# Sixteen K tiles by Strassen in the head projections, weight sums of 1024 columns, and the decode step's dot products split between VectorE and ScalarE

## The chip, the cores and the metric

The kernel runs as one program on one core of a Trainium2 chip. The metric is device time in microseconds for one execution, inputs and outputs in HBM. Three timed executions of the kernel before gave 2168.1, 2169.01 and 2167.59 us; their median, 2168.1 us, is what a change is measured against. Engines are named as in the profile: PE (matmul), PEld (its weight load), DVE (VectorE), ACT (ScalarE), POOL (GpSimd, which here mostly issues transfers), SP (which issues the weight transfers).

## The reference, cut to what matters

One inference step of a two-layer trunk, for a prompt of 512 positions and 8 single decode positions that share all weights. All 520 positions go through the same projections; width is 2048, so K is 16 tiles of 128.

```
h = RMSNorm(x);  z = h @ W_in                     # 2048 x 8192, split into 8 parts of 1024
B, C, xc, g_conv | q, k, v, g_ret = split(z)
y_conv = B * conv3(C * xc) * silu(g_conv)
q, k = rope(q), rope(k) / 16                      # 4 heads of 256
o_n = sum_{m<=n} gamma^(n-m) (q_n . k_m) v_m      # prompt, in chunks
S = gamma * S + k^T v ;  o = q @ S                # each of 8 decode positions, its own state S (256 x 256 a head)
y_ret = GroupNorm(o) * silu(g_ret)
x = x + concat(y_conv, y_ret) @ W_out
x = x + sigmoid(x @ W_pg) * (p @ W_ple)           # then the next layer; a final RMSNorm at the end
```

The outputs are y for both groups and the new convolution and retention states. Everything is float32.

## The kernel before, in words

**Products.** float32 accuracy is had from three fp32r matmuls: an operand is split into a high part and a remainder, and `mm3` (L247 to L249) adds high x high, high x low and low x high in PSUM. Activations are kept transposed, 520 columns a tile, in two halves of 260; one such product is three matmuls of 128x128 weights and 260 columns. The high part of a weight is made by ACT (L229, a copy), the remainder by DVE (L230, a subtraction), both into a ring `split` of 60 column tiles of 128; the raw weights come by SP into a ring `raw` of 32 tiles.

**Pairs of output tiles.** Every projection is done two output tiles at a time. `plain` makes 16 K tiles x 2 output tiles x 2 halves x 3 = 192 matmuls. `strassen` treats s of the 16 K tiles (s even, q = s/2) as 2x2 blocks: two output tiles, two halves of K, two halves of the columns. It makes seven products of q tiles instead of eight, and does the other 16 - s tiles plainly at the end (the loop over `chunks(s, KT)`). Its seven products read weights directly or sums of weights; four sums a pair are made on DVE, in place in the raw ring (`add`, L319), in pieces of at most `CHA` = 4 tiles, so 512 columns. The parts of each product are split in pieces of at most 4 tiles. Where s is under 16 a fourth PSUM bank `c` is held for the plain tail and the second product is copied into it by ACT; with s = 16 that copy goes straight to the output slot, and there is one ACT copy fewer. The activation-side sums are made once per stage, four DVE operations of 260 columns for two K tiles (`operand_sums`), and split; they are built a few at a time between pairs.

**Stages.** In each of the two layers: 16 pairs for the four heads (q, k, v and gate of each), 16 for the convolution branch, 8 for W_out, 8 for W_pg (7 in the last layer, where the last two tiles are done in another form). The tables `HEADS`, `CONVS`, `OUT_ROWS` and `GATES` give s for each pair; the host packs the weights' K tiles in the order that s asks for. In the heads of layer 0 the first four pairs have s = 0, 0, 0 and 8, in layer 1 the first has 0; all other head pairs have 14, most convolution pairs 16.

**Beside the products.** In the heads, DVE does the rotation (L752 to L757), and pieces of the prompt's retention run through `later` and `middle`, small queues of closures that each pair empties at fixed points. The decode step is cut into 64 pieces, one for each layer, head and decode position: `sample_load` fetches the state (128 x 512) and the rows k and q spread over all partitions, `sample_step` scales the state by gamma on ACT (L776), adds k times v on DVE (L780, two halves of 256), writes the state out (L781), and takes the dot product of each half with q on DVE (L784: one multiply that also sums, and a read of the accumulator), into `osum`. `osum` is needed at the end of the convolution stage (`sample_norm`).

**Order.** The program is written in the order of its source; a scheduler then places the instructions of each engine by its own simulated times and by priorities (the splits and weight sums have a raised one). Each engine carries out its list in order. What an engine's list looks like is therefore read from the built program, and times from the trace.

Of the kernel before, what the change touches and what calls it, by code (L numbers as in the profile page):

```python
# [9 lines left out]
AF = mybir.ActivationFunctionType  # L10
ALU = mybir.AluOpType
MUL, ADD, SUB = ALU.mult, ALU.add, ALU.subtract

P = 128
# [3 lines left out]
SEQ = 512  # L18
NS = 8
T = SEQ + NS  # L20
# [9 lines left out]
NSLOT = 75  # L30
CH = 4
CHS = 4
CHA = 4
CHL = 4
CK = 256
BUSY = 10**9
# [13 lines left out]
EARLY = 6  # L50


HEADS = [[0, 0, 0, 8] + [14] * 12, [0] + [14] * 15]
CONVS = [[14] * 2 + [16] * 13 + [14]] * 2
OUT_ROWS = [[0, 8, 16, 16, 16, 16, 16, 0]] * 2

MIXED, MIX = 64, [*range(8, 14), *range(8), 14, 15]
# [22 lines left out]
class Slots:  # L80
# [18 lines left out]
    def put(self, *slots):  # L99
        for t in slots:  # L100
            self.free.append(self.used.pop(id(t))[1])
# [90 lines left out]
def trunk_kernel(  # L192
# [6 lines left out]
    V, S, G, PE, DMA = nc.vector, nc.scalar, nc.gpsimd, nc.tensor, nc.sync  # L199
# [33 lines left out]
    def chunks(a, b, most=CH):  # L233

        n = (b - a + most - 1) // most
        e = [a + (b - a) * i // n for i in range(n + 1)] if n else [a]
        return list(zip(e, e[1:]))
# [52 lines left out]
    def strassen(x, src0, src1, s, step=None):  # L290
# [24 lines left out]
        def add(out, x, y, op):  # L315
            for i, j in chunks(0, q, CHA):
                n = slice(P * i, P * j)
                with tc.high_priority(offset=WPRIO):
                    V.tensor_tensor(out[:, n], x[:, n], y[:, n], op)  # L319
# [243 lines left out]
    def norm_g(l, k):  # L563
        return vec[:, 16 * l + k : 16 * l + k + 1]
# [15 lines left out]
    def gam(h):  # L580
        return vec[:, 128 + h : 129 + h]
# [8 lines left out]
    osum = const.tile([P, 2, H, NS], F32, name="osum")  # L590
# [71 lines left out]
    def from_dram(src):  # L662
        def load(k):
            t = get()
            SIDE.dma_start(t, src[k])
            return t

        return load

    xs = []  # L670
    X = Operands(HEADS[0][2:] + CONVS[0], from_dram(xT), gain=lambda k: norm_g(0, k))
    X.todo = [t for t in ((i, False, True) for i in range(max(X.rows) // 2))]
# [43 lines left out]
    for l in range(DEPTH):  # L716
# [15 lines left out]
        def copied(ps):  # L732
            t = get()
            for n, v in zip((LEFT, RIGHT), ps):
                S.activation(t[:, n], v, AF.Copy)
            banks.put(*[v for v in ps if not any(v is o for o in over)])
            return Val(put, slot=t)
# [10 lines left out]
        def rope(z0, z1):  # L748

            a, b = ((z if z.ps is None else copied(z.ps)).slot for z in (z0, z1))  # L750
            t1, t2 = get(), get()
            V.tensor_tensor(t1, a, rc, MUL)  # L752
            V.tensor_tensor(t2, a, rs, MUL)
            V.tensor_tensor(a, b, rs, MUL)
            V.tensor_tensor(t1, t1, a, SUB)  # L755
            V.tensor_tensor(b, b, rc, MUL)
            V.tensor_tensor(b, b, t2, ADD)  # L757
            put(a, t2)
            return [t1, b]

        def silu(z):
            g = get()
            times(g, z, rb)
            z.done()
            S.activation(g, g, AF.Silu)
            return g
# [7 lines left out]
        def sample_step(h, b, st, kb):  # L774

            keep(S.activation(st[:, :512], st[:, :512], AF.Identity, scale=gam(h)))  # L776
            k = kb[:, 256:512]
            for e in range(2):
                c = slice(256 * e, 256 * e + 256)
                keep(V.scalar_tensor_tensor(st[:, c], k, vs[:, h, e, b : b + 1], st[:, c], MUL, ADD))  # L780
            SIDE.dma_start(o_rets[l, h, b], st[:, :512])  # L781
            for e in range(2):
                c = slice(256 * e, 256 * e + 256)
                V.tensor_tensor_reduce(k, st[:, c], kb[:, :256], 1.0, 0.0, MUL, ADD, osum[:, e, h, b : b + 1])  # L784
            put(st, kb)

        loaded = []
# [1 line left out]
        def sample():  # L789

            if loaded:
                sample_step(*loaded.pop(0))
            if todo:
                loaded.append(sample_load(*todo.pop(0)))
# [6 lines left out]
        def head(m):  # L801
            middle.append(lambda: X.fill(MORE_HEAD, 0))
            if m // 2 % 2:
                middle.append(sample)
            zs = pair(X, wi[l], m, m // 2 - skipped)
            X.fill(MORE_HEAD, 0)
            X.need(m // 2 - skipped + 1)
            sample()
            return zs

        def aside_copy(h, i, tiles):

            for d, t in enumerate(tiles):
                SIDE.dma_start(hs[l, h, i + d], t[:, :SEQ])  # L814
            put(*tiles)

        def retain(h):

            mt = 8 * h
            qks = small.tile([P, 4, 32], F32, tag="qks", name="qks")  # L820
            G.memset(qks, 0.0)


            if l == 0 and h == 0:
                q = rope(*first[:2])
            else:
                q = rope(*head(mt))
            for d in range(2):
                S.activation(qks[:, d, :NS], q[d][:, SEQ:T], AF.Copy)
            aside_copy(h, 0, q)  # L830


            if l == 0 and h == 0:
                kf = rope(*first[2:])
            else:
                kf = rope(*head(mt + 2))
            for d in range(2):
                S.activation(qks[:, 2 + d, :NS], kf[d][:, SEQ:T], AF.Copy)
            aside_copy(h, 2, kf)
            qkt = small.tile([P, 4, 32], F32, tag="qkt", name="qkt")  # L840
            V.transpose(qkt.rearrange("p a b -> p (a b)"), qks.rearrange("p a b -> p (a b)"))
            for g in range(4):
                SIDE.dma_start(kq[l, h, :, :, 32 * g : 32 * g + 32], qkt[32 * g : 32 * g + NS])


            vf = []
            for e, z in enumerate(head(mt + 4)):
                t = z.slot if z.ps is None else copied(z.ps).slot
                V.scalar_tensor_tensor(vs[:, h, e, :], t[:, SEQ:T], 1.0 / 16, rb[:, SEQ:T], MUL, MUL)
                vf.append(t)  # L850
            aside_copy(h, 4, vf)
            todo.extend((h, b) for b in range(NS))


            gts = [silu(z) for z in head(mt + 6)]
            for e, gt in enumerate(gts):
                S.activation(gs[:, 2 * h + e], gt[:, SEQ:T], AF.Copy)
            aside_copy(h, 6, gts)
            later.extend(steps(h))
# [190 lines left out]
        for h in range(H):  # L1050
            retain(h)
# [121 lines left out]
        if not tail:  # L1173
            X = Operands(HEADS[l + 1] + CONVS[l + 1], next_in, RESERVE_NEXT, gain=lambda k, l=l: norm_g(l + 1, k))
        for m in range(0, KT - tail, 2):
# [39 lines left out]
        if tail:  # L1215
# [30 lines left out]
            for j, n in enumerate(blocks):  # L1246
                c = slice(PC * j, PC * j + PC)
# [79 lines left out]
            for j, n in enumerate(blocks):  # L1327
# [18 lines left out]
                c, q = slice(PC * j, PC * j + PC), slice(j, j + 1)  # L1346
# [132 lines left out]
```

## Time and profile before

| | |
|---|---|
| timed runs | 2168.1, 2169.01, 2167.59 us; median 2168.1 us |
| the profiled execution, first to last instruction | 2167.3 us |
| PE busy | 2147.8 us (99%), 17861 matmuls |
| DVE busy | 1896.1 us (87%), 3849 instructions |
| ACT busy | 1264.5 us (58%), 2647 instructions |
| POOL busy | 430.6 us (20%) |
| transfers | 387.31 MB, mean 179 GB/s |

The span of the profiled execution is 0.8 us under the median of the timed runs. A row that groups instructions gives the line, the engine, the operation, out<-in, how many, then busy time and the mean duration of one, then how long the engine was idle before them and what released it. On DVE and ACT the durations of neighbours overlap, so that a stretch of work is shorter than their sum; the distance from one start to the next is what an instruction costs its engine.

### The profile page before, as it was taken

The numbers are of one execution on the slowest core, as the hardware profiler recorded it, in microseconds if no ns is written. First come the engines' busy times: TensorE is split into PE (matmuls) and PEld (weight loads), VectorE is DVE, ScalarE is ACT, GpSimd is POOL, SyncE is SP. The second block draws the span as 40 slices with busy tenths as digits, with TensorE's granted clock in tenths as the row PEclk, the third lists the DMA queues.
The fourth block names the chain that finished last, engine by engine and source line by source line (L and its number), as shares of the span: only waits on it lengthen the run. The fifth ranks groups of instructions, "written<-read, shape, count | busy, mean of one in ns | idle before, by whom it ended". The sixth has DMA issues, their size and how long they took to land. (4 is left out here: it accounts for less than half of the span.)

```text
span 2167.3 us, 48178 instructions
## 1 busy us (share of the span) xinstructions
PE 2147.8 (99%) x17861; PEld 2142.1 (99%) x17861; DVE 1896.1 (87%) x3849; ACT 1264.5 (58%) x2647; POOL 430.6 (20%) x746
## 2 busy tenths in 40 slices
PE   9999999999999999999999999999999999999998
PEld 9999999999999999999999999999999999999998
DVE  8889988998999987987997988989999998879884
ACT  8656655565555655655765655565645555456565
POOL 2313222211001211200212222231111022011011
PEclk9999999999999999999999999999999999999999
DMA  8555565545543745645645566664464355566455
GB/s 288 171 175 197 181 217 184 178 157 175 158 129 118 238 156 187 215 154 160 215 144 175 172 213 191 189 209 170 151 182 149 120 158 202 176 207 200 128 164 198
DMA packets 182861, 387.31 MB, mean 179 GB/s; under 512 B 25888, under 2 KB 56352, under 8 KB 182624
## 3 DMA queue, kind: packets, MB, share of 16 engines
q1 hardware_dynamic: 128704, 212.98, 31.6%
q0 software_dynamic: 53056, 169.84, 23.8%
q8 instruction: 140, 2.29, 0.4%
q10 hardware_dynamic: 864, 1.39, 0.2%
q14 instruction: 97, 0.79, 0.1%
HBM read 318.96 MB, written 65.15 MB: 177 GB/s over the span
## 5 line engine op out<-in xcount | busy, mean ns | idle before, releaser
L247 PE MATMUL ps_g<-slot,split 128*128 128x260 f32 x5465 | 1531.6, 284 | 7.2 <-ACT slot L307 2.9
L248 PE MATMUL ps_g<-slot,split 128*128 128x260 f32 x5465 | 1534.3, 282 | 0.3 <-DVE slot L555 0.3
L249 PE MATMUL ps_g<-slot,split 128*128 128x260 f32 x5461 | 1519.9, 283 | 0.5 <-DVE split L230 0.5
L229 ACT ACTIVATE split<-raw 128x512 fp32r<-128x512 f32 (+2 forms) x1347 | 777.3, 596 | 583.1 <-DVE raw L319 213.2
L247 PEld LDWEIGHTS ps_g<-slot,split 128*128 128x128 f32 x5465 | 1024.0, 188 | 10.1 <-ACT slot L307 3.7
L248 PEld LDWEIGHTS ps_g<-slot,split 128*128 128x128 f32 x5465 | 1028.5, 188 | 0.5 <-DVE slot L555 0.5
L249 PEld LDWEIGHTS ps_g<-slot,split 128*128 128x128 f32 x5461 | 1019.8, 188 | 1.0 <-DVE split L230 1.0
L230 DVE TENSOR_TENSOR split<-raw,split 128x512 fp32r<-128x512 f32 (+2 forms) x1346 | 849.2, 652 | 172.5 <-PE ps_g L248 85.4
L319 DVE TENSOR_TENSOR raw<-raw 128x512 f32<-128x512 f32 (+1 forms) x660 | 428.9, 660 | 32.5 <-DMA raw<-wi 23.7
L307 ACT ACTIVATE slot<-ps_g 128x260 f32<-128x260 f32 x336 | 127.4, 381 | 140.6 <-PE ps_g L249 122.7
L551 ACT ACTIVATE slot<-slot 128x520 fp32r<-128x520 f32 (+1 forms) x212 | 109.2, 562 | 46.6 <-DVE slot L414 11.1
L552 DVE TENSOR_TENSOR slot<-slot,slot 128x520 fp32r<-128x520 f32 (+1 forms) x212 | 124.4, 620 | 4.1 <-ACT slot L551 3.9
L781 POOL DMA_DIRECT2D o_rets<-slot x64 | 35.3, 552 | 351.6 <-DVE slot L780 131.7
L307 DVE TENSOR_TENSOR slot<-ps_g,slot 128x260 f32<-128x260 f32 x168 | 70.9, 424 | 6.0 <-PE ps_g L249 3.7
L869 POOL DMA_DIRECT2D slot<-hs x64 | 46.2, 724 | 118.7 <-DVE split L230 42.7
L814 POOL DMA_DIRECT2D hs<-slot x64 | 35.6, 556 | 139.3 <-DVE slot L755 61.3
L780 DVE SCALAR_TENSOR_TENSOR slot<-slot,vs,slot 128x256 f32<-128x256 f32 x128 | 56.1, 481 | 4.5 <-ACT slot L776 4.3
L746 DVE TENSOR_TENSOR slot<-slot,slot 128x520 f32<-128x520 f32 x80 | 55.8, 698 | 4.7 <-DMA o_rets<-slot 3.7
L770 POOL DMA_DIRECT2D slot<-sret x64 | 35.5, 554 | 114.6 <-ACT split L229 37.3
L1058 POOL DMA_DIRECT2D slot<-x1s x76 | 40.8, 538 | 87.6 <-PE ps_g L249 27.2
L1209 POOL DMA_DIRECT2D x2s<-slot x30 | 16.4, 545 | 201.6 <-DVE slot L1204 200.6
L771 POOL DMA_DIRECT2D slot<-kq x64 | 34.9, 547 | 106.0 <-DVE slot L876 22.2
(217 smaller groups left out, 1733.8 us busy)
## 6 DMA issues: line engine op xcount, KB each, us to landing
raw<-wi SPq DMA_DIRECT2D x377, 256.0 KB, 3.9
raw<-wo SPq DMA_DIRECT2D x128, 256.0 KB, 5.4
raw<-wg SPq DMA_DIRECT2D x122, 256.0 KB, 4.1
raw<-wi SPq DMA_DIRECT2D x136, 192.0 KB, 4.0
slot<-x1s POOLq DMA_DIRECT2D x76, 260.0 KB, 5.1
slot<-sret POOLq DMA_DIRECT2D x64, 256.0 KB, 4.0
hs<-slot POOLq DMA_DIRECT2D x64, 256.0 KB, 4.0
slot<-hs POOLq DMA_DIRECT2D x64, 256.0 KB, 5.2
```

What stands on the lines that cost most here:

```text
L229: S.activation(hi, raw, AF.Copy)
L230: V.tensor_tensor(lo, raw, F(hi), SUB)
L247: PE.matmul(out, wh, xh, start=start, stop=False, skip_group_check=more)
L248: PE.matmul(out, wh, xl, start=False, stop=False, skip_group_check=more)
L249: PE.matmul(out, wl, xh, start=False, stop=stop, skip_group_check=more)
L307: fn(*args)
L319: V.tensor_tensor(out[:, n], x[:, n], y[:, n], op)
L551: keep(S.activation(hi, src[:, n], AF.Copy))
L552: V.tensor_tensor(lo, src[:, n], F(hi), SUB)
L746: V.tensor_tensor(out[:, n], v, table[:, n], MUL)
L780: keep(V.scalar_tensor_tensor(st[:, c], k, vs[:, h, e, b : b + 1], st[:, c], MUL, ADD))
L869: SIDE.dma_start(t[:, :512].rearrange("p (m n) -> p m n", m=2), src)
```

## The change

Three tables and constants, and one function.

- `HEADS`: every 14 becomes 16 (12 pairs in layer 0, 15 in layer 1). `CONVS`: the first two pairs of each layer go from 14 to 16, the last stays at 14. That is 31 pairs.
- `CHA` = 8: a weight sum is one instruction of up to 8 tiles (1024 columns), in every pair with Strassen tiles.
- `sample_step`: the new state (512 columns) is multiplied by q in one DVE operation, with q read twice, and ACT adds up each half of 256 with a copy that accumulates. The rows k and q trade places in `kb`, so that the product can be written over both.

```diff
-CHA = 4
+CHA = 8
...
-HEADS = [[0, 0, 0, 8] + [14] * 12, [0] + [14] * 15]
-CONVS = [[14] * 2 + [16] * 13 + [14]] * 2
+HEADS = [[0, 0, 0, 8] + [16] * 12, [0] + [16] * 15]
+CONVS = [[16] * 15 + [14]] * 2
...
         def sample_step(h, b, st, kb):
 
             keep(S.activation(st[:, :512], st[:, :512], AF.Identity, scale=gam(h)))
-            k = kb[:, 256:512]
+            k, q = kb[:, :256], kb[:, 256:512]
             for e in range(2):
                 c = slice(256 * e, 256 * e + 256)
                 keep(V.scalar_tensor_tensor(st[:, c], k, vs[:, h, e, b : b + 1], st[:, c], MUL, ADD))
             SIDE.dma_start(o_rets[l, h, b], st[:, :512])
+            both = kb[:, :512].rearrange("p (e d) -> p e d", e=2)
+            V.tensor_tensor(both, st[:, :512].rearrange("p (e d) -> p e d", e=2), q.unsqueeze(1).broadcast_to([P, 2, 256]), MUL)
             for e in range(2):
-                c = slice(256 * e, 256 * e + 256)
-                V.tensor_tensor_reduce(k, st[:, c], kb[:, :256], 1.0, 0.0, MUL, ADD, osum[:, e, h, b : b + 1])
+                S.activation(both[:, e], both[:, e], AF.Copy, accum_out=osum[:, e, h, b : b + 1])
             put(st, kb)
...
             for d in range(2):
-                S.activation(qks[:, d, :NS], q[d][:, SEQ:T], AF.Copy)
+                S.activation(qks[:, 2 + d, :NS], q[d][:, SEQ:T], AF.Copy)
...
             for d in range(2):
-                S.activation(qks[:, 2 + d, :NS], kf[d][:, SEQ:T], AF.Copy)
+                S.activation(qks[:, d, :NS], kf[d][:, SEQ:T], AF.Copy)
```

In the changed kernel the lines from L783 on stand one lower.

Counted over the whole built program, the matmuls of 260 columns into `ps_g` go from 16311 to 16218. The weight sums (L319) go from 520 of 512 columns and 140 of 384 to 312 of 1024, 8 of 896, 4 of 768 and 12 of 512. The splits (L229 and L230, each) go from about 1031 of 512 columns, 249 of 384 and 66 of 256 to about 1248, 32 and 4. ACT has 31 copies of PSUM to PSUM fewer and 128 accumulating copies more.

On DVE, this is the middle of a head pair of layer 1 (the pair of v of the first head), before the change. `raw` holds weights and their sums, `split` the parts that PE reads.

```order
L319 TENSOR_TENSOR raw_72<-raw_72 128x384
L230 TENSOR_TENSOR split_73<-raw_72,split_73 128x384
L230 TENSOR_TENSOR split_73<-raw_72,split_73 128x512
L230 TENSOR_TENSOR split_73<-raw_72,split_73 128x384
L319 TENSOR_TENSOR raw_72<-raw_72 128x512
L230 TENSOR_TENSOR split_73<-raw_72,split_73 128x512 x3
L230 TENSOR_TENSOR split_73<-raw_72,split_73 128x384
L319 TENSOR_TENSOR raw_72<-raw_72 128x512
L230 TENSOR_TENSOR split_73<-raw_72,split_73 128x384
L230 TENSOR_TENSOR split_73<-raw_72,split_73 128x512 x2
L230 TENSOR_TENSOR split_73<-raw_72,split_73 128x256 x2
```

And this is the same place in the changed kernel.

```order
L230 TENSOR_TENSOR split_73<-raw_72,split_73 128x512 x2
L319 TENSOR_TENSOR raw_72<-raw_72 128x1024
L230 TENSOR_TENSOR split_73<-raw_72,split_73 128x512 x6
L319 TENSOR_TENSOR raw_72<-raw_72 128x1024
L230 TENSOR_TENSOR split_73<-raw_72,split_73 128x512 x6
L319 TENSOR_TENSOR raw_72<-raw_72 128x1024
L307 TENSOR_TENSOR slot47_858_14722<-ps_g_14718,slot47_858_14722 128x260
L319 TENSOR_TENSOR raw_72<-raw_72 128x1024
```

The sums are whole, the splits have one width, and the two splits of 256 that fed the plain tail of the pair are gone.

On ACT, this is a decode step of layer 1 (the state is in slot 897) before the change, from its scaling by gamma on; L307 empties PSUM banks.

```order
L776 ACTIVATE slot24_897_15905<-slot24_897_15905,vec_74 128x512
L307 ACTIVATE ps_g_16243<-ps_g_16241 128x260
L229 ACTIVATE split_73<-raw_72 128x384
L229 ACTIVATE split_73<-raw_72 128x512 x2
L229 ACTIVATE split_73<-raw_72 128x256
L307 ACTIVATE slot35_916_16244<-ps_g_16240 128x260
```

And this is the same step in the changed kernel, where L785 is the accumulating copy.

```order
L776 ACTIVATE slot33_897_15556<-slot33_897_15556,vec_74 128x512
L229 ACTIVATE split_73<-raw_72 128x512
L776 ACTIVATE slot42_914_15869<-slot42_914_15869,vec_74 128x512
L229 ACTIVATE split_73<-raw_72 128x512 x2
L307 ACTIVATE slot35_916_15880<-ps_g_15877 128x260
L229 ACTIVATE split_73<-raw_72 128x512
L785 ACTIVATE slot45_898_15557,osum_82<-slot45_898_15557 128x256 x2
L229 ACTIVATE split_73<-raw_72 128x512
L307 ACTIVATE slot35_916_15880<-ps_g_15879 128x260
```

The two sums come six instructions behind the scaling here; over the 64 steps it is between 3 and 22. Splits and PSUM copies stand behind them.

## The prediction, made before the change was run

> **What bounds the kernel now.** I read the engines' shares first, then PE's own waits, then windows over the stages that the change touches, and last what DVE and ACT wait for there. The page's first part:
>
> ```profile
> span 2167.3 us, 48178 instructions
> PE 2147.8 (99%) x17861; PEld 2142.1 (99%) x17861; DVE 1896.1 (87%) x3849; ACT 1264.5 (58%) x2647; POOL 430.6 (20%) x746
> ```
>
> PE is busy but for 19.5 us. A busy PE may still be a slow one, so the second view is the windows (length; then busy time and instructions of PE, PEld, DVE, ACT, POOL; granted clock; DMA share). The first is the W_out and W_pg stages of layer 0, with 16 Strassen tiles; then the heads of layers 0 and 1 and the late convolution pairs of layer 0:
>
> ```profile
> 760.00:1040.00 280.00, 280.00 (x2340) 280.00 (x2338) 236.02 (x432) 154.99 (x298) 38.75 (x73) 1.00 0.53 170
> 120.00:500.00 380.00, 379.06 (x3170) 378.81 (x3169) 346.09 (x757) 225.89 (x492) 96.64 (x164) 1.00 0.58 184
> 1130.00:1530.00 400.00, 399.33 (x3339) 398.83 (x3338) 355.57 (x777) 234.37 (x518) 98.68 (x170) 1.00 0.59 185
> 520.00:680.00 160.00, 160.00 (x1338) 160.00 (x1337) 146.82 (x283) 87.41 (x175) 17.42 (x22) 1.00 0.47 143
> ```
>
> In the first window 280 us hold 2340 matmuls of 260 columns: **119.7 ns** each, at a full clock. The convolution window gives 119.6 ns, with DVE at 92%. So PE runs at its own pace in every stage, and the number of matmuls sets the time. The heads lose 0.94 us (layer 0) and 0.67 us (layer 1) of PE time in all, with DVE at 91% and 89%.
>
> How much room DVE and ACT have there is told by what they wait for. These rows are the waits of layer 1's heads, 1130 to 1530 us (total, times, longest):
>
> ```profile
> ACT split L229 <- PE ps_g L248: 30.5, 38, 2.5
> ACT split L229 <- PE ps_g L249: 14.0, 13, 2.5
> DVE split L230 <- ACT split L229: 17.4, 23, 2.9
> DVE raw L319 <- DMA raw<-wi: 16.3, 13, 3.0
> DVE slot L307 <- PE ps_g L249: 1.8, 2, 1.5
> ```
>
> ACT stands 44.5 us because PE has not yet freed a place in the split ring: the weights are ready too early, not too late. DVE's waits for ACT are partly that same wait, passed on. A ring of 60 tiles holds seven chunks of four K tiles (high and low part each), and a chunk feeds 12 matmuls, so PE has 7 x 12 x 0.1197 = 10 us of work in store when the ring is full.
>
> **The change, part by part.** *Matmuls.* A pair with 14 Strassen tiles needs 7 x 7 x 3 = 147 and a plain tail of 2 x 4 x 3 = 24, so 171; with 16 it needs 7 x 8 x 3 = 168. 31 pairs change (12 + 15 head pairs, 2 x 2 convolution pairs): 93 fewer, which is also the difference in the built program (16311 to 16218). 93 x 119.7 ns = **11.1 us off PE**. Nothing hides it: PE is what ends last, and its weight loads go along one for one.
>
> [...]
>
> *Splits and weight sums on DVE.* What one costs is the distance between starts, since durations overlap. This is DVE's timeline in a stretch without idle time:
>
> ```profile
> 399.86 0.41 DVE L784 CUSTOM_DVE_ANT_0 slot<-slot,slot 128x256 f32<-128x256 f32 x1
> 400.20 0.08 DVE L784 DVE_READ_ACCUMULATOR2_ANT osum<- 128x1 f32 x1
> 400.20 0.55 DVE L230 TENSOR_TENSOR split<-raw,split 128x384 fp32r<-128x384 f32 x1
> 400.67 0.68 DVE L319 TENSOR_TENSOR raw<-raw 128x512 f32<-128x512 f32 x1
> 401.27 0.42 DVE L784 CUSTOM_DVE_ANT_0 slot<-slot,slot 128x256 f32<-128x256 f32 x1
> ```
>
> 256 columns cost 0.34 us, 384 cost 0.47, 512 cost 0.60: 0.13 us per 128 columns and 0.08 fixed. The trace has no sum of 1024 columns; on that line it costs 0.60 + 4 x 0.13 = 1.12 us. It can hardly be under 1.04 (the columns alone) or over 1.20 (two of 512); I take 1.12.
>
> A pair that goes from 14 to 16 had splits 7 x (0.47 + 0.60) + 2 x 0.34 = 8.17 us and has 14 x 0.60 = 8.40; sums 4 x (0.47 + 0.60) = 4.28 and now 4 x 1.12 = 4.48. That is **+0.43 us of DVE a pair**, 13.3 us for 31. The 47 pairs that had 16 already save 4 x (1.20 - 1.12) = 0.32 us each, 15.0 us, and three others 1.0 us together. In the heads alone it is 27 x 0.43 = +11.6 us, over windows in which DVE was idle for 78 us of 780. PE's store of 10 us covers it; bare, it would be those 11.6 us, less what the next part gives back.
>
> *Decode steps.* By durations the part looks large:
>
> ```profile
> L784 DVE CUSTOM_DVE_ANT_0 slot<-slot,slot 128x256 f32<-128x256 f32 x128 | 53.9, 421 | 0.0
> L784 DVE DVE_READ_ACCUMULATOR2_ANT osum<- 128x1 f32 x128 | 11.1, 87 | 0.0
> L230 DVE TENSOR_TENSOR split<-raw,split 128x512 fp32r<-128x512 f32 x1031 | 695.0, 690 | 147.8 <-PE ps_g L248 81.2 <-ACT split L229 51.8 <-issue 6.1
> ```
>
> 65.0 us go and 64 x 0.69 = 44.2 come. But the timeline shows that the accumulator reads cost no distance and the products 0.34 us, so a step saves 2 x 0.34 - 0.60 = 0.08 us of DVE, 5.1 us over 64. **DVE's sum** is 13.3 - 16.0 - 5.1 = about -8 us, off the path that sets the end. The product costs like the 512-column row as both read two SBUF operands; a repeated q might be slower, at most as much as today's two halves.
>
> ACT gets 128 accumulating copies of 256 columns, which the trace does not have. The nearest rows:
>
> ```profile
> L229 ACT ACTIVATE split<-raw 128x256 fp32r<-128x256 f32 x66 | 27.3, 415 | 36.7 <-DMA raw<-wi 29.0 <-PE ps_g L248 5.2 <-PE ps_g L249 1.9
> L988 ACT ACTIVATE slot<-slot,shift,rstp 128x256 f32<-128x256 f32 x6 | 3.2, 587 | 0.0
> L307 ACT ACTIVATE ps_g<-ps_g 128x260 f32<-128x260 f32 x121 | 45.1, 373 | 16.4 <-PE ps_g L249 16.1
> ```
>
> Below, 0.415 us (a plain copy); above, 0.587 + 0.087 us (two operands of a column each, and a read as long as DVE's). I take 0.50, nearer the copy that it is: +64 us (53 to 86), less 31 PSUM copies at 0.373 = 11.6 us. ACT goes from 1264 to about 1316 us, 61% of the span. That hides behind PE as long as ACT idles 44.5 us on a full ring in one stage.
>
> *The new wait.* L785 waits on ACT for DVE's product. Queued behind it are the high parts of the splits, for which DVE's remainder and then PE wait, and the copies out of PSUM. The tightest is the copy of bank `a` behind a pair's first product: the third product writes `a` again, so it may be late by the second product, 24 x 0.1197 = 2.9 us. DVE's own chain from the last L780 (0.34 us) to the product is 3 to 8 instructions, 1.5 to 4 us, and in most steps a dozen ACT instructions of about half a microsecond lie between. A handful of the 64 will make ACT stand 1 or 2 us, under the 2.9. I take nothing for it.
>
> *A sum that starts later.* One 1024-column sum needs both halves of its weights in, and its first split comes 1.12 - 0.60 = 0.52 us later. 10 us in store cover that too, except where PE has emptied the ring. PE's waits over the whole execution show how seldom that is:
>
> ```profile
> PE ps_g L247 <- ACT slot L307: 2.9, 4, 1.3
> PE ps_g L247 <- ACT ps_g L307: 1.6, 2, 1.2
> PE ps_g L247 <- ACT split L229: 1.5, 2, 1.3
> PE ps_g L249 <- DVE split L230: 0.5, 1, 0.5
> ```
>
> Three waits for splits in 2167 us, 2.0 us. [...]
>
> *Sum:* 2167.3 - 11.1 = 2156.2 us for the profiled execution; with the 0.8 us by which the median of the runs lies over it, **2157.0 us**. The decode step's transfers stay as they are; 62 weight transfers of 128 KB for the tails go into larger ones, and the bytes stay.
>
> **The rivals.**
>
> 1. *Fewer stalls as well* (2153.7 us). DVE gets lighter outside the heads, and the waits above (6.5 us for copies and splits) could shrink. For it: the convolution stages lose 0.32 us a pair. Against it: most of these waits stand at changes of stage, where the chain goes through ACT and transfers. Half of the 6.5 us gone is 3.3 us more.
>
> 2. *The heads empty the ring now and then* (2161 us). DVE's work per head pair rises by 0.43 us while PE's falls by 0.36. In bursts, such as a rotation (six operations of 520 columns, 0.61 us each on the line above) beside a wide sum that starts late, the 10 us run out. If a third of DVE's 11.6 us more in the heads gets through to PE, 3.9 us of the gain go back. For it: layer 1 already waits 16.3 us for weights. Against it: 44.5 us of ACT waiting on PE.
>
> 3. *ACT's queue blocks* (2167 us, no change). If the accumulating copies stop ACT long enough that PE loses 0.17 us a step, 64 x 0.17 = 11 us, the gain is gone. For it: 64 new waits in an in-order queue. Against it: L307's waits on PE's side come to 4.5 us today, though L776 and others wait in the same queue.
>
> 4. *DVE becomes the pace of all changed pairs* (2176 us, slower). Then the 93 matmuls buy nothing, and a changed pair costs DVE's 0.43 us: 13.3 - 5.1 = +8.2 us. It decides from the point where DVE has no idle time left in the heads: 44.4 of 400 us in layer 1 would have to be bound elsewhere. For it: of DVE's own waits there only the 1.8 us of L307 are on PE. Against it: the 92% window of the convolution, where pairs of 16 run at 119.6 ns.
>
> 5. *The change doesn't do what it says*: excluded for the matmuls, which are counted in the built program.
>
> **How the numbers follow.** The forecast (2156 to 2158.5) has 0.65, rival 1 has 0.10, rival 2 0.14, rival 3 0.07, rival 4 0.04. A measurement of this kernel tells about 0.2%, 4.3 us, from no change: faster is under 2163.8 us, slower over 2172.4. Faster is the forecast, rival 1 and nearly all of rival 2: 0.88. Same is rival 3 and the rest of rival 2: 0.08. Slower is 0.04. The range reaches from half of rival 1 (2154.5) to the bulk of rival 2 (2161.5); some 2 in 10 lie outside.
>
> **What would show it.** Right: PE busy near 2137 us and its idle time still near 19 us; windows in the heads with 119.7 ns a matmul; sums of 1024 columns with starts 1.12 us apart; DVE's busy time lower by about 8 us; ACT about 50 us busier. Wrong: PE waits on L229, L230 or L307 in the heads that total over 5 us (rival 2 or 3, by the line named), ACT idle before L785 for over 2.9 us at a time, or ACT's waits on PE in the heads gone (rival 4).

## The result and the profile after

The changed kernel took 2201.47 us (median of four runs, 2194.72 to 2206.27) against 2168.56 us before: a ratio of **1.0153**, 95% interval 1.0133 to 1.0173. Forecast was 2157.0 us. The change is slower by 33 us where it was to be faster by 11. Two single executions in the experiments below, one of e3 (4245 us) and one of d3 (2304 us), were in a slow state, and the medians given here are of the others.

The first lines of the page of the kernel after:

```profile
span 2200.2 us, 46804 instructions
PE 2156.1 (98%) x17768; PEld 2141.9 (97%) x17768; DVE 1898.6 (86%) x3271; ACT 1280.9 (58%) x2810; POOL 433.0 (20%) x746
```

The 93 matmuls are gone (17861 to 17768), and yet PE is busy 8.3 us longer and idle 44.1 us in place of 19.5. The three longest of PE's waits in the kernel after, whole execution (total, times, longest), name the engines:

```profile
PE ps_g L247 <- ACT slot L307: 13.6, 15, 3.0
PE ps_g L247 <- ACT split L229: 10.9, 13, 1.6
PE ps_g L249 <- DVE split L230: 4.7, 10, 0.6
```

Before, these were 2.9, 1.5 and 0.5 us. The windows that were shown of before, in the kernel after (length; busy time and instructions of PE, PEld, DVE, ACT, POOL; clock; DMA share):

```profile
120.00:500.00 380.00, 372.68 (x3072) 369.40 (x3071) 343.15 (x587) 229.97 (x530) 97.33 (x163) 1.00 0.55 182
1130.00:1530.00 400.00, 388.83 (x3193) 384.40 (x3193) 352.66 (x592) 236.65 (x540) 100.13 (x170) 0.99 0.56 183
520.00:680.00 160.00, 159.50 (x1328) 159.05 (x1328) 146.43 (x237) 90.66 (x208) 13.96 (x25) 1.00 0.46 146
```

The first two are the heads: 380 us of layer 0 now hold 3072 PE instructions where they held 3170, and 400 us of layer 1 hold 3193 in place of 3339. At 119.7 ns each that is 12.3 and 17.8 us lost, where it was 0.6 and 0.3. The convolution window loses 10 instructions, some 1 us. A second place lies behind the stages that the prediction looked at: the windows from the W_out stage of layer 1 to the end, of the kernel before and then of the one after, whose last 33 us are its longer time.

```profile
1760.00:2167.00 407.00, 396.32 (x3294) 394.93 (x3292) 327.57 (x622) 229.38 (x478) 68.30 (x126) 1.00 0.56 184
```

```profile
1760.00:2200.00 440.00, 424.25 (x3468) 421.70 (x3466) 344.10 (x611) 237.07 (x501) 74.73 (x128) 0.98 0.53 175
```

By the same price 12.7 us were lost there before and 24.9 after. So of the 44 us to be found (32.9 us between the profiled executions, and the 11.1 us of matmuls that were saved) the heads took 29.2 and this stretch 12.2. A single stall shows how, in lines of the timeline of the kernel after around 1240 us (lines between them are left out):

```profile
1239.76 1.67 ACT L229 ACTIVATE split<-raw 128x512 fp32r<-128x512 f32 x3 [2.07 <-DMA raw<-wi]
1240.44 0.39 PE L247 MATMUL ps_g<-slot,split 128*128 128x260 f32 x1 [1.57 <-ACT split L229]
1241.34 0.40 ACT L785 ACTIVATE slot<-slot 128x256 f32<-128x256 f32 x1
1241.74 0.40 ACT L785 ACTIVATE slot<-slot 128x256 f32<-128x256 f32 x1
1242.26 0.67 ACT L307 ACTIVATE slot<-ps_g 128x260 f32<-128x260 f32 x2
1242.98 0.58 PE L247 MATMUL ps_g<-slot,split 128*128 128x260 f32 x1 [2.03 <-ACT slot L307]
1243.36 0.42 PE L248 MATMUL ps_g<-slot,split 128*128 128x260 f32 x1
1243.58 0.42 PE L249 MATMUL ps_g<-slot,split 128*128 128x260 f32 x1
```

PE finds no split weights and waits 1.57 us. The first line's bracket says where this began: ACT itself had stood idle for 2.07 us until a transfer of raw weights landed. ACT then has three splits, two accumulating copies and only behind them the copy that frees PE's next PSUM bank, and PE waits another 2.03 us. From there the matmuls start 0.22 us apart instead of 0.12. Windows around that place show the granted clock with it (the third number from the right):

```profile
1232.00:1239.00 7.00, 6.88 (x58) 6.64 (x57) 6.43 (x12) 4.89 (x9) 1.33 (x2) 1.00 0.78 244
1239.00:1243.00 4.00, 0.53 (x3) 0.32 (x3) 3.65 (x7) 3.13 (x9) 0.73 (x1) 0.77 0.87 298
1243.00:1250.00 7.00, 7.00 (x40) 7.00 (x40) 5.56 (x10) 1.38 (x5) 1.71 (x4) 0.64 0.36 133
```

Behind the two waits, 3.6 us together, the granted clock is 0.64 in the mean of 7 us, which hold 40 matmuls where the 7 us ahead of the waits held 58. Other stalls begin at a transfer too. If each of PE's waits is followed back for 8 us through the waits of the engines in front of it, 9.9 of 35.8 us in the kernel after begin at late weights and 10.2 at other transfers; in the kernel before it is 2.0 and 3.3 of 11.2. These are estimates.

By kind, the 32.9 us are made up like this. Matmuls: -11.1. Idle time of PE: 44.1 - 19.5 = +24.6. Clock: its mean is 0.994 after and 0.999 before, so (1 - 0.994) x 2200 - (1 - 0.999) x 2167 = 13.2 - 2.2 = +11.0, an estimate. The clock's own records in the traces bear it out: half the clock was granted in the kernel after for 3.4 us from 162.5, 1804.4 and 1831.7 us on, for 6.8 us from 1241.2 and 2145.7 us on, and at the very end; in the kernel before at the very end alone. That is 13.6 us lost (1.4 of them while PE was idle anyway) against 1.6. The rest, 8.4, lies in PE's busy time, and the waits give it a size: the first matmul behind the wait above takes 0.39 us where the pace is 0.12, 0.27 more, and the times in PE's whole list of waits add up to 51 where they were 18; 33 x 0.27 = 8.9. That one matmul is typical: over the 34 waits that lie clear of each other and of the half clock, PE's busy time grows by 0.27 us a wait (median).

### The profile page after: what moved, and what is told of

It is laid out like the page before. It is cut to its first block, busy times and chain, and to the rows that moved or that the text cites. A ratio compares the mean times of both kernels' runs of the same rounds, so it can differ in the third digit from the quotient of the medians.

```text
span 2200.2 us, 46804 instructions
## 1 busy us (share of the span) xinstructions
PE 2156.1 (98%) x17768; PEld 2141.9 (97%) x17768; DVE 1898.6 (86%) x3271; ACT 1280.9 (58%) x2810; POOL 433.0 (20%) x746
## 5 line engine op out<-in xcount | busy, mean ns | idle before, releaser
L247 PE MATMUL ps_g<-slot,split 128*128 128x260 f32 x5434 | 1531.3, 285 | 29.2 <-ACT slot L307 13.6
L229 ACT ACTIVATE split<-raw 128x512 fp32r<-128x512 f32 (+1 forms) x1285 | 751.5, 620 | 489.4 <-PE ps_g L249 181.1
L230 DVE TENSOR_TENSOR split<-raw,split 128x512 fp32r<-128x512 f32 (+1 forms) x1284 | 837.5, 681 | 216.1 <-ACT split L229 119.6
L319 DVE TENSOR_TENSOR raw<-raw 128x1024 f32<-128x1024 f32 (+2 forms) x336 | 400.9, 1193 | 7.4 <-DMA raw<-wi 3.5
L307 ACT ACTIVATE slot<-ps_g 128x260 f32<-128x260 f32 x336 | 127.5, 381 | 202.7 <-PE ps_g L249 173.6
L307 DVE TENSOR_TENSOR slot<-ps_g,slot 128x260 f32<-128x260 f32 x168 | 70.6, 421 | 11.3 <-PE ps_g L249 11.3
L785 ACT ACTIVATE slot<-slot 128x256 f32<-128x256 f32 x128 | 51.6, 405 | 10.8 <-DVE slot L783 8.1
```

The lines of the kernel that those rows point to most:

```text
L229: S.activation(hi, raw, AF.Copy)
L230: V.tensor_tensor(lo, raw, F(hi), SUB)
L247: PE.matmul(out, wh, xh, start=start, stop=False, skip_group_check=more)
L307: fn(*args)
L785: S.activation(both[:, e], both[:, e], AF.Copy, accum_out=osum[:, e, h, b : b + 1])
```

## The experiments

Medians are given against the runs of the kernel before on the same chip, 2168 to 2169 us; a difference is to that.

**The three parts, each alone, and the change without its wide sums.** Three theories stood: the wide sums (W), 16 tiles in the heads (R), ACT's queue (S).

```diff
e1  HEADS, CONVS as in the change; CHA = 4, sample_step as before
e2  CHA = 8; the rest as before
e3  sample_step and qks as in the change; the rest as before
e4  the change with CHA = 4
```

> The tables of rows alone (31 pairs from 14 to 16 tiles), sums in pieces of 512 and the decode step as before. 93 matmuls fewer are worth 11.1 us. Theory W (the wide sums empty the split ring: a sum of 1024 columns, then ACT's high part, then DVE's remainder stand in a row before PE has work): no stall from this part, 2157 us, PE gaps as before. Theory R (16 tiles in the heads are too much for DVE beside the rotation and the retention): 2185 us or more, with gaps in 80 to 420 and 1120 to 1500 us and the half clock behind them. Theory S (the accumulating copies block ACT's queue): 2157 us.

> The weight sums of 1024 columns alone. No matmul goes. Theory W: 2185 us or more, since all 47 pairs of 16 tiles and the 384+512 pairs of the heads get the long chain. Theory R: 2168 us (no change), as DVE's work falls by some 15 us. Theory S: 2168 us.

> The decode step alone: one product on DVE, two accumulating copies on ACT. No matmul goes. Theory W and theory R: 2168 us, no change. Theory S: 2185 us or more, with PE waiting for L307 and L229 on ACT behind the accumulating copies.

> The change without its wide sums: tables and decode step, sums in pieces of 512 columns. Theory W: the whole gain stands, 2157 us. Theory R: 2185 us or more, as DVE's work in the heads is no less than with rows alone but for 5 us. Theory S: 2185 us or more.

| run | median us | ratio, 95% interval |
|---|---|---|
| e1, rows alone | 2187.83 | 1.0089, 1.0071 to 1.0107 |
| e2, wide sums alone | 2189.85 | 1.0102, 1.0087 to 1.0118 |
| e3, decode step alone | 2175.09 | 1.0031, 1.0017 to 1.0045 |
| e4, rows and decode step | 2182.75 | 1.0069, 1.0052 to 1.0086 |

Each part is slower alone: +19.6, +21.6 and +6.8 us. No theory stands as a single cause: W falls with e1 and e4, R with e2, S covers 7 us. PE's waits also differ in kind. For splits (L229 and L230) PE waits 2.5 us in the kernel before, 9.1 with rows alone and 15.6 in the change, but only 3.5 with wide sums alone. There the copies out of PSUM (L307) grew, from 4.7 to 9.9 us, and waits of other kinds from 4.1 to 10.1. Two rows of e2:

```profile
PE ps_g L247 <- ACT slot L307: 7.3, 10, 2.4
PE ps_g L247 <- ACT split L229: 1.4, 2, 0.8
```

The profile of e1 also upsets a reading. This is a row of ACT's waits in the heads of layer 1 (1130 to 1530 us), with rows alone:

```profile
ACT split L229 <- PE ps_g L249: 50.9, 45, 6.3
```

And this is the window over the same stretch:

```profile
1130.00:1530.00 400.00, 391.87 (x3256) 389.27 (x3255) 363.21 (x732) 224.45 (x460) 99.42 (x170) 1.00 0.57 185
```

ACT waits on a full ring for 50.9 us, more than the 44.5 of before, and in the same 400 us PE is idle for 8.1 us. A ring that is often full is no proof that it is never empty.

**Is it the order?** The scheduler places every instruction anew for each edit. Two edits that change no work (null edits) were made on both kernels.

```diff
n1, n3 (strassen)
-        z0, z1 = get(), get()
+        z1, z0 = get(), get()
n2, n4 (sample_step)
-            put(st, kb)
+            put(kb, st)
```

> The kernel before, with nothing of the change: the two output slots of a Strassen pair are taken in the other order (z1 before z0), so they swap places in memory. Same instructions, same sizes, same counts; in the built program 898 of 3851 DVE instructions and 717 of 2655 ACT instructions stand elsewhere. Theory O (the order on the engines: the order of before is a lucky one, and whatever moves it brings stalls of PE): 2175 to 2190 us, with PE gaps in the heads. Theory P (each part of the change has a price of its own in work or waits): 2168 us, within 4 us.

> The kernel before, with the two slots of a decode step given back in the other order (kb before st). Same work; 312 of 3851 DVE and 141 of 2655 ACT instructions stand elsewhere. Theory O: 2172 to 2185 us, less than the run above as less moves. Theory P: 2168 us, within 4 us.

> The changed kernel, with z1 taken before z0. Same work as the changed kernel; 845 of 3273 DVE instructions stand elsewhere. Theory O: another time than 2201 us, off by more than 5 us either way. Theory P: 2201 us, within 5.

> The changed kernel, with kb given back before st. Same work; 302 of 3273 DVE instructions stand elsewhere. Theory O: off 2201 us by more than 5 us, or not, but the four null edits together spread over 10 us or more. Theory P: 2201 us, within 5.

| | as it is | z1 before z0 | kb back first |
|---|---|---|---|
| kernel before | 2168.56 | 2187.04 (1.0091, 1.0067 to 1.0114) | 2167.80 (0.9999, 0.9990 to 1.0009) |
| kernel after | 2201.47 | 2226.11 (1.0272, 1.0256 to 1.0287) | 2210.34 (1.0192, 1.0175 to 1.0210) |
| difference | +33 | +39 | +43 |

Two slots that trade places cost 19 us on the kernel before and 25 on the one after, with not one instruction more; the other null edit costs nothing on the one and 9 us on the other. So a single comparison on this kernel carries some 20 us of order. And yet the change costs 33 to 43 us in all three columns, and the slowest of the three kernels before (2187 us) is 14 us faster than the fastest of the three after: in these orders it has a price of its own besides. In n3, PE's waits tell where the order hurts:

```profile
PE ps_g L247 <- ACT slot L307: 18.3, 15, 4.1
PE ps_g L249 <- DVE split L230: 14.0, 21, 1.9
```

The change with the slots exchanged waits longer for the same copies (13.6 us in the change as it is) and three times as long for low parts (4.7 us there).

**How much does DVE's work in the heads matter?** Four of the six operations of each rotation were left out, so that q and k are not rotated.

```diff
-            t1, t2 = get(), get()
+            t1 = get()
             V.tensor_tensor(t1, a, rc, MUL)
-            V.tensor_tensor(t2, a, rs, MUL)
-            V.tensor_tensor(a, b, rs, MUL)
-            V.tensor_tensor(t1, t1, a, SUB)
-            V.tensor_tensor(b, b, rc, MUL)
-            V.tensor_tensor(b, b, t2, ADD)
-            put(a, t2)
+            V.tensor_tensor(b, b, rs, MUL)
+            put(a)
```

> The kernel before with four of the six DVE operations of each rotation of q and k left out (two of 520 columns stay, so q and k are not rotated): 64 operations of 0.61 us, 39 us of DVE in the heads, 4.9 us a head. PE's work is the same. It is the control for the next three: 2166 to 2170 us by every theory but the order (up to 2187 by that alone).

> The tables of rows alone, with the same four operations of each rotation left out. Theory D (DVE has too little spare time in the heads: with 16 tiles its work for one matmul rises by 4 to 5%, and the store of split weights runs dry): the gain comes, 11 us under the control, about 2157 us, and the stalls of the heads (22 us with the full rotation) go. Theory L (it is the chain of sum, high part, remainder and PSUM copy through two in-order engines, not DVE's work): still 2180 us or more.

> The sums of 1024 columns alone, with the same four operations left out. Theory D: near the control, within 5 us. Theory L: 15 to 20 us over the control, with stalls outside the heads too (690 to 780 and 1760 to 1850 us).

> The whole change, with the same four operations left out. Theory D: about 2157 us, 11 us under the control. Theory L: 2190 us or more. Both in part: rows give their 11 us, wide sums take 15 to 20, so 2172 to 2180 us.

| with the light rotation | median us | against the light kernel before |
|---|---|---|
| kernel before (d1) | 2173.26 | |
| rows alone (d2) | 2174.21 | +1.0 (with the full rotation +19.6) |
| wide sums alone (d3) | 2192.41 | +19.2 (+21.6) |
| the change (d4) | 2193.22 | +20.0 (+33) |

The two parts behave differently. Counted with the 11.1 us of matmuls that they save, the rows cost 30.7 us with the full rotation and 12.1 when DVE has 4.9 us less to do in each head. That is what theory D says in part: their 11 us still do not come. PE idles 29.0 us in d2 and 26.1 in d1 (span less busy time of one execution each; that of d1 took 6 us over its median). The price of the wide sums does not care (theory L). But leaving out work moves instructions too: d1 has less to do and is 5 us over the kernel before, so order may have a part in these differences.

**Where the wide sums cost, and how deep the store is.** For this the lead was worked out: for each low part, the time from the end of its subtraction (L230) in the trace to the start of the first matmul that reads that place of the ring, which the built program gives. In us, the median and, behind the stroke, the value that a tenth of the parts fall short of:

| kernel | heads, layer 0 (80 to 500) | convolution (520 to 690) | W_out, W_pg (780 to 1050) | heads, layer 1 (1150 to 1500) |
|---|---|---|---|---|
| before | 7.8 / 4.7 | 3.4 / 2.0 | 7.6 / 5.0 | 6.1 / 2.7 |
| after | 5.7 / 2.0 | 3.3 / 1.1 | 7.2 / 3.6 | 6.0 / 1.8 |
| rows alone | 6.8 / 2.7 | 3.2 / 1.4 | 7.7 / 5.1 | 6.0 / 2.2 |
| wide sums alone | 6.9 / 2.9 | 3.0 / 1.0 | 7.3 / 3.5 | 6.1 / 2.2 |
| before, z1 before z0 (n1) | 6.3 / 2.2 | 3.2 / 1.8 | 7.1 / 4.6 | 5.4 / 2.0 |
| after, z1 before z0 (n3) | 4.0 / 0.9 | 3.2 / 1.3 | 7.4 / 3.6 | 3.7 / 0.9 |

PE's store is nowhere 10 us: 3 to 8 us, with dips to half of that and less. The wide sums take 1.0 to 1.8 us off its dips in three of the four stages and 0.5 in the last, and the rows 2.0 in the heads of layer 0. The dips do not say by themselves where time is lost, though. They are deepest in the convolutions, where the kernel after loses 1 us. With wide sums alone the heads of layer 0 lose 0.7 us (3169 matmuls in 380 us) at dips of 2.9, and those of layer 1 lose 10.4 us (3255 in 400) at dips of 2.2. Four runs tested whether the depth decides (theory T).

```diff
f1, f2 (strassen, L294 and L316)
-        q = s // 2
+        q, cha = s // 2, (CHA if x.gain else 8)     # f1: wide in W_out and W_pg only
+        q, cha = s // 2, (8 if x.gain else CHA)     # f2: wide in heads and convolutions only
-            for i, j in chunks(0, q, CHA):
+            for i, j in chunks(0, q, cha):
f3 (before)
-SPLIT = 60
+SPLIT = 52
f4 (e4: rows and decode step)
-SPLIT = 60
+SPLIT = 64
```

> The kernel before with sums of 1024 columns only in the W_out and W_pg stages (22 pairs), where the splits lie some 7 to 8 us ahead of PE. Theory T (a wide sum delays the next split by some 1.5 us, and that costs only where the store is thin): no change, 2168 us within 5. Theory O (order): up to 20 us either way, with stalls in the heads, which the edit does not touch.

> The kernel before with sums of 1024 columns (896 where s is 14) only in the heads and the convolution pairs, where the splits lie 3 to 8 us ahead with dips under 3. Theory T: all of the 20 us that the wide sums cost alone, 2183 to 2192 us, with the stalls in the heads of layer 1 and at the ends of the convolution stages. Theory O: anything from 2168 to 2190 us.

> The kernel before with a ring of 52 split tiles in place of 60: the same work, a store that is one chunk (1.4 us) shallower. Theory T (depth decides): 2180 us or more, the stalls in the heads. If depth does not matter but order does: anything, with no tie to the stages where the store is thin.

> Rows and decode step without wide sums (2182.8 us with a ring of 60), with a ring of 64: half a chunk, 0.7 us, deeper. Theory T: fewer stalls in the heads, 2165 to 2177 us. Theory O: between 2165 and 2200 us, with no direction.

| run | median us | ratio, 95% interval |
|---|---|---|
| f1, wide in W_out and W_pg | 2170.69 | 1.0008, 0.9998 to 1.0018 |
| f2, wide in heads and convolutions | 2188.84 | 1.0088, 1.0067 to 1.0109 |
| f3, before with 52 tiles | 2197.19 | 1.0131, 1.0116 to 1.0146 |
| f4, rows and step with 64 tiles | 2192.27 | 1.0100, 1.0083 to 1.0117 |

The first three went as T says. In f1 the dips of the lead fall from 5.0 to 3.1 us in the stages that were edited, and no time is lost: the same sums are free there. Nearly all of the price is in f2. And one chunk off the ring, with the same instructions, costs 28 us; PE's waits in f3:

```profile
PE ps_g L247 <- ACT slot L307: 10.3, 10, 2.4
PE ps_g L247 <- ACT split L229: 8.2, 10, 1.4
```

Both are the waits that the change made longer too (13.6 and 10.9 us there). None of the three excludes the order (theory O), since each edit also moved instructions. ACT's list has 2647 entries in all of these kernels; compared place by place in the traces (line, operation, names and shape), it differs from that of the kernel before in 265 places in f1 and 320 in the null edit n2, which are both free, in 566 in n1 (+19 us), and in 1017 in f2 and 1603 in f3. The two edits that cost 20 and 28 us are also those that moved most. (d1 moved 983 places and costs 5 us, with less to do.)

f4 went against T: it is 9.5 us slower than e4. The ring of 64 made the dips of the lead shallower in the convolutions (1.2 us in e4, 3.2 in f4) and in the heads (2.2 and 1.5 us in e4, 2.8 and 2.7 in f4; 2.7 is also the value of the kernel before in layer 1), and the stalls in the heads stayed. PE is idle there for 8.3 us in layer 0 and 10.1 in layer 1, whose window is:

```profile
1130.00:1530.00 400.00, 389.87 (x3215) 386.14 (x3214) 356.41 (x662) 236.93 (x537) 98.91 (x170) 1.00 0.58 181
```

The largest of PE's waits in f4, 10.0 us in 11 times, is for copies out of PSUM (L307). A ring of weights does not shorten that queue: the copies stand in ACT's list behind whatever was placed there first.

**Can the rows' gain come anywhere?** The rows were divided by the pairs' kind.

```diff
g1  (v and gate pairs, first convolution pairs: 18 pairs)
+HEADS = [[0, 0, 0, 8] + [14, 14, 16, 16] * 3, [0, 14, 16, 16] + [14, 14, 16, 16] * 3]
+CONVS = [[16] * 15 + [14]] * 2
g2  (q and k pairs: 13 pairs)
+HEADS = [[0, 0, 0, 8] + [16, 16, 14, 14] * 3, [0, 16, 14, 14] + [16, 16, 14, 14] * 3]
```

> Rows alone, of 16 tiles, only in the v and gate pairs of the heads and in the first two convolution pairs: 18 pairs, 54 matmuls, 6.5 us of PE. Theory D (the loss sits where DVE has the rotation to do): the gain comes, 2162 to 2166 us. Theory O (order): anywhere from 2162 to 2190 us.

> Rows alone, only in the q and k pairs of the heads: 13 pairs, 39 matmuls, 4.7 us of PE. Theory D: all of the loss of the rows, 2182 to 2190 us, with the gaps in 80 to 420 and 1120 to 1500 us. Theory O: anywhere from 2163 to 2190 us, with no tie to the run before.

g1 took 2175.84 us (1.0039, 1.0024 to 1.0054), g2 2194.67 us (1.0119, 1.0103 to 1.0136). g1 loses 14 us against its 6.5 us of saved matmuls, g2 31 us against 4.7. That the q and k pairs, beside which DVE rotates, are the worse half fits theory D; that g2 is slower than both halves together (e1, 2187.83) does not, and the 7 us between them are within what order alone did above. None of the eighteen kernels was faster than the kernel before by more than its interval.

## Why the prediction was wrong, point by point

*What bounds the kernel.* Right: PE at 119.7 ns a matmul. In the W_out and W_pg stage of the kernel after, 280 us hold 2334 matmuls, 120.0 ns each:

```profile
760.00:1040.00 280.00, 280.00 (x2334) 279.83 (x2333) 228.81 (x382) 147.47 (x292) 38.64 (x72) 1.00 0.53 174
```

*Matmuls, 11.1 us.* Right in count, and the account of the 32.9 us above closes with it. The gain was there and was more than spent.

*Splits and sums on DVE.* The prices were right: sums of 1024 columns are 1219 ns long and start 1.14 us before the next instruction (foreseen 1.12). Rows alone raise DVE's busy time by 23.6 us; with sums of 512 columns the prediction's prices give 31 x (0.23 + 0.52) = 23.3. But DVE's busy time as a whole rose by 2.5 us where 8 less were foreseen: wide sums alone lower it by 14.6, and the decode step by 2.6 (5.1 foreseen). These sizes are off, but DVE's busy time is not what decided.

*Decode step.* An accumulating copy is 405 ns long and its read, a row of its own, 188 ns; two copies start 0.40 us apart, under the 0.50 that was taken:

```profile
L785 ACT ACTIVATE slot<-slot 128x256 f32<-128x256 f32 x128 | 51.6, 405 | 10.8 <-DVE slot L783 8.1 <-DMA o_rets<-slot 1.6 <-ACT split L229 1.0
```

ACT stood 8.1 us on DVE's products in all, the "handful" of short waits that was foreseen. In e3 ACT is 49.3 us busier (1313.8 us), below the 64 (53 to 86) that 128 copies were priced at. In the change it is only 16.4 busier, where some 50 were foreseen: rows alone take off 9.6 us (11.6 foreseen, for 31 PSUM copies), and wide sums alone 17.5, which the prediction left out. In e2 ACT's instructions are the same 2647; their durations add up to 3 us less, so most of the 17.5 is that they overlap more. "I take nothing for it" was wrong by 6.8 us (e3), and n1 shows that order alone can do as much.

*The cover.* **This is the step that failed**: "PE has 7 x 12 x 0.1197 = 10 us of work in store when the ring is full", and "PE's store of 10 us covers it". The ring is not full when it matters. In the kernel before the lead is 7.8 and 6.1 us in the heads by the median, and a tenth of the splits come with under 4.7 and 2.7. The 44.5 us that ACT waits on PE were read as slack, and e1 shows them at 50.9 beside stalls: an average over a window in which the store swings. The rows that were shown for this were also a choice. In the same window of the kernel before, ACT's splits waited longer for the other side, for weight sums and raw weights:

```profile
ACT split L229 <- DVE raw L319: 37.9, 32, 3.6
ACT split L229 <- DMA raw<-wi: 26.9, 24, 3.5
```

That is 64.8 us against 44.5, so "the weights are ready too early, not too late" was half of what the view says. In the heads of the kernel after, PE's waits on L229, L230 and L307 come to 17.3 us, where the prediction had named 5 as a sign of being wrong. The two terms set to nothing on the ground of the full ring, DVE's 0.43 us a pair in the heads and the sum that starts 0.52 us later, belong to the parts that cost some 20 us each in e1 and e2. They failed in different ways. With rows alone PE waits for splits, 9.1 us in place of 2.5: the store ran out. With wide sums alone it waits 3.5 us for splits, and more for copies out of PSUM, which a store of weights does not cover. That the wide sums come to this through ACT's list, where late splits hold up the copies behind them, is likely from the stall at 1240 us but not shown. With a light rotation the first price falls, and with the wide sums moved to W_out and W_pg the second goes, but order may have a part in both.

*A sum that starts later.* The three waits for splits that were shown for it, 2.0 us, are not all: PE's whole list has a fourth, 0.5 us in `ps_r`. e2, with the longer sums alone, is 21.6 us slower, but what PE's waits grew by there is mostly of another kind (for splits they are 3.5 us in place of 2.5), and what part of it is order is not known.

*What stands behind a stall.* Nothing was said of it. In the kernel after PE's busy time grows by 0.27 us a wait (the median above), and half the clock was granted for 3.4 or 6.8 us at five places before the end. By the account above the two added 19.4 us (8.4 in busy time, 11.0 by the clock) to the 24.6 of idle time.

*The rivals.* Rival 2 (the heads empty the ring now and then) is the mechanism in part; it was foreseen at 3.9 us, and the rows alone cost a multiple of that. Rival 4 set the slower side at 2176 us, from DVE as the pace; DVE was busy for 90% and 88% of the heads after, so it was never the pace in the mean. Rival 3's place (ACT's queue in front of L307) shows in 13.6 us of waits, but the queue is not blocked by the accumulating copies alone: e1 and e2, which have none, wait 6.3 and 7.3 us there. No rival named the order as such, which moves this kernel by up to 25 us.

*What stays open.* How the 33 us divide between the order that the scheduler happened to find and the change's own price is not known; the change cost 33 to 43 us under three orders. No run holds the order fixed while the depth of the store changes, so that the depth decides is argued, and f4 speaks against it. Late transfers were not tested as a cause: over the whole execution ACT's splits wait less for weights from `wi` in the kernel after (53.8 us) than before (75.6), but some of PE's stalls begin there. Why a ring of 64 did not help the heads was not settled beyond the waits on L307. Whether some order would let the rows' 11 us come was not found.

## What to carry to other kernels

Less work for an engine that is busy for 99% of the time need not be a gain: with 11.1 us of matmuls less, the rows alone took 19.6 us more. Ask whether those that feed it stay ahead at their worst moments: a feeder's waits on a full buffer may stand beside an empty one (in e1 50.9 us of such waits in 400 us, in which PE was idle for 8.1). Read all of a feeder's waits, those for its own inputs too, and every kind of wait of the busy engine: here copies out of PSUM cost it about as much as missing weights (13.6 and 15.6 us in the kernel after). How far ahead the fed data lie (the low tenth, by stage) shows how thin the cover is, but did not tell alone where time is lost. Before a difference of one or two per cent is put down to an edit in a scheduled program, make a null edit, such as two buffers that trade places, and see what the order alone does (here up to 25 us). A longer instruction on a helper engine can cost more than it saves in busy time: here 20 us in the heads and convolutions (f2) and nothing in W_out and W_pg (f1).

## What was not expected of the hardware

Two waits of PE, 1.57 and 2.03 us with two matmuls between them, are followed by matmuls 0.22 us apart, where the pace is 0.12, and by 7 us with a mean granted clock of 0.64. Over the whole execution the mean clock is 0.994 in the kernel after and 0.999 in the one before. In the kernel after the granted clock was halved five times before its end, for 3.4 or 6.8 us; in the 3.4 us ahead of each halving PE had been busy for 30 to 51% (48% at 1241 us), and the longest single wait in PE's list is 3.0 us.
